# A row roll on one core: the last 256 rows copied in DMAs of half a row per engine

## The chip, the cores and the metric

The kernel runs on one core of a Trainium2 chip. The metric is the device time in microseconds; lower is better. The kernel does almost no computing (in the profile before, VectorE is busy for 1% of the span and GpSimd for 4%): it moves an array within device memory, and 16 DMA engines do the work (each DMA of the copy has 16 landings in the trace). SyncE and ScalarE (SP and ACT in the profile) only issue DMAs; the page lists no busy time for either.

## The reference

```python
x = np.random.randn(8192, 8192).astype(np.float32)
shift = 100
def reference(x, shift):
    return np.roll(x, shift, axis=1)
```

Each row of 32 KiB moves right by 100 elements, and the last 100 elements come round to the front.

## The kernel before

Columns 256 to 8191 of the output (7936 elements, 31744 B per row) are copied straight from input to output. The loop below issues this. The first 256 columns go through on-chip memory on GpSimd's queue.

```python
    engines = [nc.sync, nc.scalar]
    # ... (cut; the comments here and below are the document's)
    # here s = 100, a = 256, g = a - s = 156
    xm = x.rearrange("(c e j) w -> c j e w", e=16, j=4)
    om = out.rearrange("(c e j) w -> c j e w", e=16, j=4)
    if a < n_cols:
        for c in range(n_rows // 64):
            for j in range(4):
                engines[j % 2].dma_start(out=om[c, j, :, a:], in_=xm[c, j, :, g:n_cols - s])
    # ... (the first 256 columns, through GpSimd's queue)
```

Each DMA has an outer dimension of 16. 512 such DMAs are issued, 256 per queue, and the trace has 8192 packets of 31744 B for them and 16 landings for each DMA. This document reads that as one row for each of the 16 DMA engines, though the records do not name the engines. In the trace the 512 DMAs use eight semaphores in turn, 64 DMAs each. All but the first eight wait for their own semaphore, and each of these starts 0.016 to 0.021 us after the last of the 16 landings of the DMA before it on that semaphore. So **eight DMAs are under way** at most. This document calls that the window. Its width in bytes is eight times what one DMA holds.

## Time and profile before

| | kernel before |
|---|---|
| median of the first three runs | 821.17 us (819.21 to 822.31) |
| span of the profiled run | 818.3 us |
| rate in the second half of the span, the last two slices of 40 left out | 326 to 341 GB/s |
| a DMA, issue to landing, median | 12.6 us |
| a row on one engine with its semaphore write, mean; the quickest row alone | 1.477 us; 1.173 us |

The prediction below shows the lines and reads them. The *skew* of a DMA is the time from its first landing to its last: the trace records 16 landings for each DMA, up to 8.1 us apart in the last 16 DMAs of the kernel before. The *end* is the end of the last data packet, 1.3 to 1.9 us before the end of the span in all traces.

### The profile page before, as it was taken

Reading aid. Unit: us, or ns where it says so; the run is one execution under the profiler, and the core shown is the slowest. Engines: PE = TensorE matmul, PEld = TensorE weight load, DVE = VectorE, ACT = ScalarE, POOL = GpSimd, SP = SyncE. Lnnn points to the kernel's source line nnn. Section 1 sums busy time; section 2 is a strip of 40 time slices with the busy share of each in tenths; the row PEclk is TensorE's granted clock in tenths of the full one; section 3 lists DMA queues with packets and bytes.
Section 4 is the critical chain, followed back from the end, with each engine's and each line's share of the span. In section 5 each row is a group of like instructions: output and inputs, shape, how many; then the busy total and the mean of one; then the engine's idle time right before and its main releaser. Section 6 shows DMA issues by size and latency. Waiting matters only on the chain. (4 is left out here: it accounts for less than half of the span.)

```text
span 818.3 us, 617 instructions
## 1 busy us (share of the span) xinstructions
DVE 7.7 (1%) x8; POOL 28.8 (4%) x40
## 2 busy tenths in 40 slices
DVE  0000000000000000000000000000000000000000
POOL 3000000000000000000000000000000000000000
DMA  9999999999999999999999999999999999999997
GB/s 313 343 345 352 338 352 342 363 338 358 349 342 352 354 355 352 348 364 357 337 335 341 327 335 334 326 332 334 338 337 334 330 334 334 332 327 334 334 321 262
DMA packets 21060, 276.89 MB, mean 338 GB/s; under 512 B 8768, under 2 KB 8768, under 8 KB 12864
## 3 DMA queue, kind: packets, MB, share of 16 engines
q10 hardware_dynamic: 8192, 130.04, 46.4%
q1 hardware_dynamic: 8192, 130.04, 46.0%
q0 software_dynamic: 4672, 16.78, 6.8%
q14 instruction: 4, 0.03, 0.0%
HBM read 268.44 MB, written 268.44 MB: 656 GB/s over the span
## 5 line engine op out<-in xcount | busy, mean ns | idle before, releaser
L77 POOL DMA_DIRECT2D out_dram<-h x16 | 13.2, 825 | 197.8 <-DMA out_dram<-h 112.6
L68 POOL DMA_DIRECT2D t<-in_x_dram x12 | 9.5, 793 | 59.7 <-DMA h<-in_x_dram 30.0
L70 DVE COPY h<-t 128x1200 f32<-128x1200 f32 x4 | 3.1, 786 | 232.3 <-DMA t<-in_x_dram 173.4
L73 DVE COPY h<-t 128x1872 f32<-128x1872 f32 x4 | 4.9, 1224 | 0.0
L69 POOL DMA_DIRECT2D h<-in_x_dram x4 | 3.0, 748 | 45.4 <-DMA t<-in_x_dram 45.4
L72 POOL DMA_DIRECT2D h<-in_x_dram x4 | 3.0, 750 | 41.7 <-DMA t<-in_x_dram 41.7
L94 POOL MEMSET const-float32-0.0<- 128x1 f32 x1 | 0.1, 98 | 0.2 <-issue 0.2
L94 POOL MEMSET const-bfloat16-1.0<- 128x1 bf16 x1 | 0.1, 102 | 0.0
L94 POOL MEMSET const-uint8-127<- 128x1 uint8 x1 | 0.1, 99 | 0.0
L94 POOL MEMSET const-float32-1.0<- 128x1 f32 x1 | 0.1, 98 | 0.0
## 6 DMA issues: line engine op xcount, KB each, us to landing
out_dram<-in_x_dram ACTq DMA_DIRECT2D x256, 496.0 KB, 12.6
out_dram<-in_x_dram SPq DMA_DIRECT2D x256, 496.0 KB, 12.6
out_dram<-h POOLq DMA_DIRECT2D x16, 512.0 KB, 113.7
t<-in_x_dram POOLq DMA_DIRECT2D x12, 512.0 KB, 94.9
h<-in_x_dram POOLq DMA_DIRECT2D x4, 312.0 KB, 92.1
h<-in_x_dram POOLq DMA_DIRECT2D x4, 200.0 KB, 97.4
```

Source lines behind the costliest of these rows:

```text
L68: nc.gpsimd.dma_start(out=t[:, q - 1], in_=lead)
L69: nc.gpsimd.dma_start(out=h[:, Q - 1, :, :s], in_=xt[k, Q - 1, :, :, n_cols - s:])
L70: nc.vector.tensor_copy(h[:, :Q - 1, :, :s], t[:, :, :, :s])
L72: nc.gpsimd.dma_start(out=h[:, 0, :, s:], in_=xt[k, 0, :, :, :g])
L73: nc.vector.tensor_copy(h[:, 1:, :, s:], t[:, :, :, s:])
L77: nc.gpsimd.dma_start(out=ot[k, q, :, :, :a], in_=h[:, q])
L94: nc = _bacc.Bacc("TRN2", target_bir_lowering=False, num_devices=1)
```

## The change

It is meant to level the finish. In the profiled run of the kernel before, eight engines end from 811.2 to 812.7 us, and the other eight still have rows to move until 814.7 to 816.8 us. Smaller DMAs at the end are meant to let the quick engines run ahead by less.

The diff is shown without its unchanged lines.

```diff
-        for c in range(n_rows // 64):
+        blocks = n_rows // 64
+        mid = (a + n_cols) // 256 * 128
+        for c in range(blocks):
+            parts = ((a, mid), (mid, n_cols)) if c >= blocks - 4 and a < mid else ((a, n_cols),)
             for j in range(4):
-                engines[j % 2].dma_start(out=om[c, j, :, a:], in_=xm[c, j, :, g:n_cols - s])
+                for lo, hi in parts:
+                    engines[j % 2].dma_start(out=om[c, j, :, lo:hi], in_=xm[c, j, :, lo - s:hi - s])
```

## The prediction

Its sum: -0.9 us for the more level end and +0.3 us for the packets, -0.6 us together. Its 8 ns per packet are the estimate from the quickest packets in the trace (158 ns for 4096 B, 1173 ns for 31744 B); its 2.3 us fixed are one from the 4.7 us to the first landing, less two packets. The 1 us per turn of the window under rival 2, and with it 824.5 us, is the author's guess; no trace gives it.

> **What bounds the kernel now.** I read the page first, then the longest waits of the SyncE queue, then the issues of the copy loop (line 38), and last the stretches of the end.
>
> ```profile
> span 818.3 us, 617 instructions
> ...
> DMA  9999999999999999999999999999999999999997
> GB/s 313 343 345 352 338 352 342 363 338 358 349 342 352 354 355 352 348 364 357 337 335 341 327 335 334 326 332 334 338 337 334 330 334 334 332 327 334 334 321 262
> ...
> q10 hardware_dynamic: 8192, 130.04, 46.4%
> q1 hardware_dynamic: 8192, 130.04, 46.0%
> q0 software_dynamic: 4672, 16.78, 6.8%
> ```
>
> The DMA engines are busy in 39 of 40 slices, and the compute engines do next to nothing, so the transfers are the bound. In the last half, where only the copy loop moves data, the rate is 326 to 341 GB/s. The last slice alone has holes: 7 tenths and 262 GB/s. The change touches only what happens there and shortly before. The two hardware queues hold 8192 packets each; by size these are 4096 rows of 31744 B and 4096 semaphore writes of 4 B, so a whole row is one packet. Its mean time is (46.4% + 46.0%) x 818.3 us x 16 engines / 8192 rows = 1.477 us. The packet records give 1.173 us for the quickest, so a row takes a quarter longer while all 16 engines run than it could.
>
> ```profile
> SPq L38 <- DMA out_dram<-in_x_dram: 670.4, 252, 3.9
> SPq L108 <- DMA out_dram<-in_x_dram: 10.7, 4, 3.1
> ...
> L38 ACTq DMA_DIRECT2D out_dram<-in_x_dram x256: 516/517/828, 0.7 to 806.0; - x128
> L38 SPq DMA_DIRECT2D out_dram<-in_x_dram x256: 509/510/627, 0.7 to 805.8; - x128
> ...
> DMA to landing us min/median/max: 5.6/12.6/14.9
> ```
>
> The queue waited 252 times, which is 256 issues less the first four. The order of instructions says why: each DMA waits for one of eight semaphores, four on SyncE's queue and four on ScalarE's, so exactly eight DMAs are under way. Two of them, one per queue, are finished every 3.1 us or so, hence the 12.6 us from issue to landing. Issue costs 0.51 us of these 3.1, and the sequencer is not the bound.
>
> ```profile
> core 0: us, DVE busy (x) POOL busy (x), PEclk, DMA share, GB/s
> 794.00:800.00 6.00, 0.00 (x0) 0.00 (x0) 1.00 1.04 328
> 800.00:806.00 6.00, 0.00 (x0) 0.00 (x0) 1.00 1.01 339
> 806.00:811.20 5.20, 0.00 (x0) 0.00 (x0) 1.00 0.93 317
> 811.20:812.80 1.60, 0.00 (x0) 0.00 (x0) 1.00 0.65 278
> 812.80:814.70 1.90, 0.00 (x0) 0.00 (x0) 1.00 0.43 184
> 814.70:816.80 2.10, 0.00 (x0) 0.00 (x0) 1.00 0.18 76
> 816.80:818.30 1.50, 0.00 (x0) 0.00 (x0) 1.00 0.00 0
> ```
>
> This is the tail that the change aims at. The landing records show that every DMA has its 16 landings spread out: in the last 50 us the first comes some 5 us after the issue and the last some 12.7 us after it, a skew of 6.2 to 8.2 us. Chaining the packets end to start gives each engine's own end: eight engines end from 811.2 to 812.7 us, the other eight from 814.7 to 816.8 us. Summed over the engines that is 42.6 engine-us of idling, 2.66 us of the whole machine. After 812 us the packets left take 1.175 us each, the quickest time: with half the engines silent, the rest run at full speed. The last four pairs of DMAs land 3.2, 2.4 and 2.3 us apart, where 3.1 was usual before.
>
> [...]16 landings per DMA, up to 8 us apart, and the next issue starts 0.02 us after the last one. So the eight-DMA window moves at the pace of the slowest engine, and limits how far a quick one can run ahead.
> [...]the quickest 4096 B packet took 158 ns, the quickest 31744 B packet 1173 ns, so (1173 - 158) / 27648 B is 0.0367 ns per byte, and 158 - 150 leaves about 8 ns per packet.
> [...]both queues' DMAs of a pair land 0.2 us apart on the slow engines.
> [...]16 engines at 31744 B per 1.173 us would be 433 GB/s, and the steady copy makes 335. Something shared holds the engines back, and that is what decides what a more level finish is worth.
>
> **The change, part by part.** *Removed:* the last 16 DMAs of 496 KB (8 per queue). *Added:* 32 DMAs of 248 KB (16 per queue). The bytes, their order, the queue of each row and the addresses stay. The split falls at 4224, so both halves are 3968 elements, 15872 B. The order of instructions shows the same eight semaphores in the same turn. The part concerned is 256 rows x 31744 B = 8.13 MB, 24.3 us at 335 GB/s, so about from 792 us to the end; nothing before that changes.
>
> *Cost, packets.* Each engine gets 16 more data packets at 8 ns and 16 more semaphore writes, whose median record is 9 ns: 16 x 17 ns = 0.27 us, on the path of the slowest engine.
> *Cost, issues.* 16 x 0.51 us = 8.2 us per queue within 24 us, where a DMA is due every 1.55 us. Hidden.
> *Cost, thinner window.* Eight half DMAs are 8 x 15872 B per engine; on a slow engine that is 8 x 0.78 = 6.2 us of work. When the oldest pair lands there, three pairs, 4.6 us, are still queued. The first packet of the program starts 1.4 us after the first issue, so a new DMA reaches it in time and the slow engine never starves. Cost 0.
> *Gain, tail.* The lead of a quick engine is bounded by the window. Issue to first landing now is 4.7 us or so, of which two packets are 2.4 us and the rest 2.3 us fixed; with halves that is 2.3 + 1.2 = 3.5 us, against 6.2 us for the slowest. So the skew should fall from 6 to 8 us to about 2.7 us, and the 5.6 us from the first engine's end to the last's to about half. What is a fully level end worth? From 811.2 to 816.8 us the engines work (5.6 - 2.66) x 16 = 47 engine-us, which at 1.175 us is 40 rows. All 16 engines at 1.477 us per row do 10.8 rows per us, 3.7 us for the 40: a level end would come 1.9 us sooner. Half the skew: 0.9 us sooner.
> *Sum:* -0.9 + 0.3 = -0.6 us, if the quick engines' new idling costs nothing. Before the end everything stands, and from the last packet to the end of the span is 1.5 us both times. So 821.2 - 0.6 = 820.6; I choose 820.5.
>
> **The rivals.**
> *1. The idling is only moved.* To lose 3 to 5 us of lead, the quick engines must sit idle during those 24 us, waiting for the window, instead of after 811 us. If they all idle at once, the slow ones run at 1.175 us a row then and at 1.477 us at the end, the same sum in another order. For it: the quick engines are a group of eight that ends within 1.5 us, so they would likely stall together. Against: over short stretches the stalls need not coincide, and up to a fifth of the engines could be idle without the shared limit loosening (335/433 is 0.77). It makes the time 821.2 + 0.3 = 821.5.
> *2. The window becomes the bound.* If a new DMA takes much longer than 1.4 us to reach the engines under load (quick engines show 2.3 us fixed in all)[...], halving what is queued starves the slow engines too. Losing 1 us for each of the four turns of the window, the estimate is +3 to +4 us, 824.5. Against: 4.6 us are queued behind each landing.
> *3. Short packets level the sharing.* The two groups may owe their difference to how packets of 31744 B compete; shorter ones could bring all 16 engines to one pace, and the whole 1.9 us would come: 819.5. Nothing speaks for it beyond the level start, where the skew is 0.5 us.
>
> **Range and chances.** The spread of these is 819 to 824.5 us, with most weight at 820 to 821.5. The three times of the kernel before run from 819.21 to 822.31 us, so noise of 1.5 us either way is larger than the effect. I take 817.5 to 823.0. Two per cent are 16.4 us: faster by that is impossible by the sum above, as the whole idle tail is 2.66 us; slower needs the last 24 us to grow by two thirds. Chances: 1% faster, 98% within, 1% slower.
>
> **What would show it.** In the changed kernel: 248 issues per queue of 496 KB and 16 of 248 KB; issue to landing of the halves 6 to 7 us; skew in the halves 2.5 to 4 us; first to last engine's end under 4 us and the rate before the end unchanged at 320 to 340 GB/s. If the DMA share of the 20 us before the tail sinks below 0.95 while the tail gets shorter, rival 1 is right. If the rate of that stretch sinks below 310 GB/s and the span grows, rival 2. If the halves' engines end within 1 us at an unchanged rate, rival 3. The prediction is wrong if the times leave 817.5 to 823.0, or if the skew of the halves stays at 6 us or more, because then the window does not set it.

## More of the kernel before

All runs told here are at a granted clock of 1.0. Chips differ more than kernels do: the kernel before took 820 to 821 us on two chips and 830 to 831 us on two others (medians). So a kernel is compared only with runs of the kernel before on the same chip in the same rounds.

## The result and the profile after

The changed kernel took 819.87 us in the median of six runs (818.34 to 820.66). The kernel before took 820.99 us in six runs (818.13 to 822.31). The ratio is 0.9989 with a 95% interval of 0.9969 to 1.0009. Ratios here are the mean time of one kernel's fast runs over that of the other's in the same rounds, so not quite the ratio of the medians. Within 2%, as predicted, and not clear of zero.

The page of the changed kernel, with the busy tenths of the DMA engines and their rate in 40 slices:

```profile
span 817.9 us, 633 instructions
...
DMA  9999999999999999999999999999999999999998
GB/s 307 333 348 342 347 355 347 355 356 344 350 338 363 359 351 354 361 346 360 334 333 341 326 335 331 331 332 337 328 338 331 330 336 331 335 334 326 331 308 299
```

Look at the last two slices. In the kernel before they read 321 and 262 GB/s; here they read 308 and 299. The last slice gained and the one before it lost.

The issues, with count, size and median time from issue to landing, and the longest waits of SyncE's queue:

```profile
out_dram<-in_x_dram ACTq DMA_DIRECT2D x248, 496.0 KB, 12.7
...
out_dram<-in_x_dram SPq DMA_DIRECT2D x16, 248.0 KB, 5.7
out_dram<-in_x_dram ACTq DMA_DIRECT2D x16, 248.0 KB, 5.9
```

```profile
SPq L43 <- DMA out_dram<-in_x_dram: 671.1, 259, 3.9
SPq L113 <- DMA out_dram<-in_x_dram: 5.3, 4, 2.0
```

The halves land after 5.7 and 5.9 us, less than half of the 12.7 us of the whole rows: the window is half as wide, eight times 248 KB instead of eight times 496 KB. The waits at the very end (line 113 here, 108 before) fell from 10.7 to 5.3 us.

Now the same stretches counted back from the end in both kernels. The columns are the stretch, its length, busy time of the compute engines, clock, share of the DMA engines, and GB/s. A packet counts wholly in the stretch in which it starts, so a share can pass 1. The kernel before:

```profile
core 0: us, DVE busy (x) POOL busy (x), PEclk, DMA share, GB/s
784.80:790.80 6.00, 0.00 (x0) 0.00 (x0) 1.00 1.01 323
790.80:798.80 8.00, 0.00 (x0) 0.00 (x0) 1.00 0.94 294
798.80:808.80 10.00, 0.00 (x0) 0.00 (x0) 1.00 1.00 337
808.80:812.80 4.00, 0.00 (x0) 0.00 (x0) 1.00 0.83 310
812.80:816.80 4.00, 0.00 (x0) 0.00 (x0) 1.00 0.30 127
```

The changed kernel:

```profile
784.60:790.60 6.00, 0.00 (x0) 0.00 (x0) 1.00 0.97 317
790.60:798.60 8.00, 0.00 (x0) 0.00 (x0) 1.00 0.79 278
798.60:808.60 10.00, 0.00 (x0) 0.00 (x0) 1.00 0.94 346
808.60:812.60 4.00, 0.00 (x0) 0.00 (x0) 1.00 0.99 337
812.60:816.60 4.00, 0.00 (x0) 0.00 (x0) 1.00 0.74 242
```

The hole of the last 4 us is largely filled: the share went from 0.30 to 0.74. A new hole opened where the whole rows turn into halves, at 790 to 799 us, with a share of 0.79. The reading is that the quick engines wait there for the slow ones, because the narrower window no longer lets them stay ahead; e3 and e6 below test it.

### The profile page after: what moved, and what is told of

It is laid out like the page before. It is cut to its first block, busy times and chain, and to the rows that moved or that the text cites. A ratio compares the mean times of both kernels' runs of the same rounds, so it can differ in the third digit from the quotient of the medians.

```text
span 817.9 us, 633 instructions
## 1 busy us (share of the span) xinstructions
DVE 7.7 (1%) x8; POOL 28.9 (4%) x40
## 6 DMA issues: line engine op xcount, KB each, us to landing
out_dram<-in_x_dram ACTq DMA_DIRECT2D x248, 496.0 KB, 12.7
out_dram<-in_x_dram SPq DMA_DIRECT2D x248, 496.0 KB, 12.7
```

## The experiments

Twelve runs were made, all with the right result; five of them are one of the two kernels again. In the diffs, `...` marks lines that are cut. Each value in the table below is from one profiled execution. For e6 the skew is that of the row DMAs alone. "Idle" is time in which the 16 engines had no data packet, averaged over the engines, by the packet records (semaphore writes are left out). "Last 12 MB" is how long before the end 12 MB were still to be moved.

| run | skew of the last 8 DMAs (median) | idle, 40 to 8 us before the end | idle, last 8 us | last 12 MB |
|---|---|---|---|---|
| before, three traces | 6.7, 6.4, 6.7 us | 0.4, 0.5, 0.1 us | 2.9, 3.3, 3.8 us | 39.1, 38.6, 39.9 us |
| changed, first three traces | 1.5, 1.7, 1.8 us | 2.2, 1.2, 1.4 us | 0.8, 0.6, 1.0 us | 37.7, 37.3, 37.8 us |
| e3: half packets, wide window | 5.1 us | 0.1 us | 3.0 us | 39.0 us |
| e6: whole packets, narrow window | 2.2 us | 3.1 us | 1.6 us | 39.7 us |
| e5: halves in the last 128 rows | 2.1 us | 1.4 us | 1.3 us | 37.8 us |
| e2: quarters | 1.6 us | 6.4 us | 2.0 us | 45.1 us |

### e0: the changed kernel again

No edit.

> The changed kernel once more, for a closer interval. My theory after the first look: the eight-DMA window sets the skew between engines; halving it makes the quick engines idle between about 790 and 800 us instead of after 811 us, and only a part of the tail's 2.7 us of idling is won. Ratio to before 0.9985 to 0.9995 (819.8 to 820.6 where before is 821), last engines ending within 1 to 2 us of each other. Rival, all of the gain is noise: 1.000 with the interval on both sides of it.

Measured: 831.31 us against 830.36, ratio 1.0014 (0.9995 to 1.0033). The trace has the expected shape, with a small skew and a hole before the end, but the total time shows no gain on this chip.

### e3: half-size packets, window as wide as before

The change does two things at once: it halves the packet, and it halves the bytes under way. This run does only the first. Each DMA holds two half rows per engine, from two neighbouring rows.

```diff
...
+                if c < blocks - 4:
+                    engines[j % 2].dma_start(out=om[c, j, :, a:], in_=xm[c, j, :, g:n_cols - s])
+                    continue
+                at = (c * 64 + j // 2 * 2) * n_cols + j % 2 * w    # w = 3968
+                engines[j % 2].dma_start(
+                    out=bass.AP(tensor=out.tensor, offset=at + a, ap=[[4 * n_cols, 16], [n_cols, 2], [1, w]]),
+                    in_=bass.AP(tensor=x.tensor, offset=at + g, ap=[[4 * n_cols, 16], [n_cols, 2], [1, w]]))
```

> The last 256 rows in packets of half a row, but two packets per engine and DMA, so that a DMA stays 496 KB and the window stays as wide as in the kernel before. Theory (the window sets the skew, not the packet): skew of the landings stays 5.5 to 8 us, the engines end some 5 us apart, time as before (+0.1 to +0.3 us for 16 more packets). Rival (short packets level the sharing among the engines): skew of 1 to 2.5 us and a level end, as the changed kernel shows.

The stretches of 18 to 8, 8 to 4 and 4 to 0 us before its end:

```profile
811.10:821.10 10.00, 0.00 (x0) 0.00 (x0) 1.00 0.99 333
821.10:825.10 4.00, 0.00 (x0) 0.00 (x0) 1.00 0.96 329
825.10:829.10 4.00, 0.00 (x0) 0.00 (x0) 1.00 0.20 83
```

The tail is that of the kernel before: a share of 0.20 in the last 4 us, 3.0 us of idling in the last 8 us, and a skew of 4.6 to 6.5 us in the last eight DMAs, a little under the 5.5 to 8 us expected. Half-size packets alone do not level the end. The time was 831.93 us, ratio 1.0021 (1.0005 to 1.0038). That is 0.4 to 3.1 us more (0.0005 and 0.0038 times 830.4), where 0.1 to 0.3 us was expected. Why it should be more I did not find out.

### e6: whole packets, narrow window

The opposite. Between two row DMAs a DMA of 512 B per engine takes up a semaphore, so four row DMAs are under way, as many bytes as eight halves. In its trace these row DMAs landed 7.5 us after the issue in the median, where the last whole rows of the kernel before took 12.7 us.

```diff
...
+        sp = spare.tile([16, 16 * 128], x.dtype)
...
                 engines[j % 2].dma_start(out=om[c, j, :, a:], in_=xm[c, j, :, g:n_cols - s])
+                if c >= blocks - 4:
+                    engines[j % 2].dma_start(out=sp[:, n * 128:n * 128 + 128], in_=xm[c, j, :, 0:128])
+                    n += 1
```

> The last 256 rows in whole-row packets, but between two of them a DMA of 512 B per engine that nobody reads, which takes up one of the eight semaphores: four row DMAs under way instead of eight, as many bytes as eight halves. Theory (window): skew of the last row DMAs 2 to 3.5 us, engines end within 2.5 us, holes in the DMA share before the tail; time between 819.5 and 821.5. Rival (packet size): skew stays 5.5 us or more, time as before or a little over.

The stretches of 26 to 18, 18 to 8, 8 to 4 and 4 to 0 us before its end:

```profile
802.20:810.20 8.00, 0.00 (x0) 0.00 (x0) 1.00 0.72 265
810.20:820.20 10.00, 0.00 (x0) 0.00 (x0) 1.00 0.93 310
820.20:824.20 4.00, 0.00 (x0) 0.00 (x0) 1.00 1.04 365
824.20:828.20 4.00, 0.00 (x0) 0.00 (x0) 1.00 0.45 155
```

The hole before the end and a more level end are there with whole packets: 1.6 us of idling in the last 8 us, against 2.9 to 3.8 us in the kernel before. The last eight row DMAs have a skew of 0.9 to 3.6 us. With e3 this settles which of the two counts here: **the bytes in the window set the skew, not the packet.** The skew does not simply follow the bytes, though: halves brought it from 6.4 to 6.7 us down to 1.5 to 2.1 us, and quarters (e2) left it at 1.6 us. The time was 831.68 us, ratio 1.0016 (1.0002 to 1.0030), somewhat worse than expected. The engines were idle for 3.1 us before the tail, against 1.1 to 2.2 us with halves; that this ate up what the tail gave fits the numbers, but was not tested apart.

### e2: quarters of a row

```diff
-            parts = ((a, mid), (mid, n_cols)) if c >= blocks - 4 and a < mid else ((a, n_cols),)
+            parts = [(a + i * w, a + i * w + w) for i in range(4)] if c >= blocks - 4 else [(a, n_cols)]  # w = 1984
```

> The last 256 rows in quarters of a row: 64 DMAs of 124 KB. Theory: eight of them are 8 x 7936 B per engine, some 3.1 us of work at the shared pace, while a DMA needs at least about 2.9 us from issue to its first landing on an idle engine; a turn of the window takes some 3.8 us, 267 GB/s instead of 335, so 30 us for the 8.13 MB instead of 24 us, less 1 to 2 us for a level end: 824 to 827 us, share of the DMA engines 0.6 to 0.8 over the last 30 us. If the window is still wide enough, the time is 820 to 821 and the engines end within 1 us.

Its quarters in the view of the issues, and the stretch of 18 to 8 us before its end:

```profile
out_dram<-in_x_dram SPq DMA_DIRECT2D x32, 124.0 KB, 4.0
```

```profile
817.00:827.00 10.00, 0.00 (x0) 0.00 (x0) 1.00 0.83 260
```

Measured: 836.99 us against 830.36, ratio 1.0079 (1.0060 to 1.0098). A turn of the window took 4.0 us, where 3.8 was expected, and the rate fell to 260 GB/s. Here the window is the bound: at the 333 GB/s of the copy, eight DMAs of 124 KB would turn in 3.1 us, and they took 4.0. The expectation's 2.9 us to the first landing is the prediction's 2.3 us plus two quarters of a row; the last eight quarters had theirs after 2.6 us in the median. The cost, 6.5 us by the ratio, is a little over the 3 to 6 us expected. This is rival 2 of the prediction, one halving further on. That halves are still wide enough is shown by e1 below, where the rate holds; a window's bytes over its landing time can't show it, because that quotient gives about the rate itself whether or not the window is the bound.

### e1: all rows in halves

```diff
-            parts = ((a, mid), (mid, n_cols)) if c >= blocks - 4 and a < mid else ((a, n_cols),)
+            parts = ((a, mid), (mid, n_cols)) if a < mid else ((a, n_cols),)
```

> All 8192 rows in halves, so the thin window holds all the way: no lead is built up and there is no change from one window to the other. Theory (something that the engines share is the bound, and idle engines cost nothing while a few at a time are idle): share of the DMA engines 0.94 to 0.97 throughout, rate as before, engines end within 2 us; the 512 more packets and semaphore writes per engine, 512 x 17 ns = 8.7 us, are hidden in that slack: ratio 0.998 to 1.004. Rival (the slowest engines are the bound, each packet's cost is on the path): 8.7 us more and some 1 us won at the end, ratio 1.008 to 1.012.

The stretches 400 to 600 and 600 to 780 us, in e1:

```profile
400.00:600.00 200.00, 0.00 (x0) 0.00 (x0) 1.00 0.99 333
600.00:780.00 180.00, 0.00 (x0) 0.00 (x0) 1.00 1.00 332
```

In the kernel before:

```profile
400.00:600.00 200.00, 0.00 (x0) 0.00 (x0) 1.00 1.00 334
600.00:780.00 180.00, 0.00 (x0) 0.00 (x0) 1.00 1.00 333
```

The rate is the same within 1 GB/s. The ratio was 1.0020 (0.9994 to 1.0045), 822.85 us against 820.27. The 8.7 us of added packets and semaphore writes, an estimate from the trace before (512 times 17 ns: 8 ns per packet and 9 ns per semaphore write, its median), would be 1.0106. The upper end of the interval is 3.7 us, or 5.3 us if the 1.6 us that a level end is worth in the last 12 MB (below) are added back, so a good part of them is hidden. The share was expected to fall to 0.94 to 0.97; it stayed at 0.98 to 0.99 over most of the run by the packet records.

Two more things are in e1's trace. Between 400 and 780 us the median skew of its DMAs is 1.9 us, where the kernel before has 5.9 us: the window holds the engines together all the way, not only at the end. And one thing changed that was not meant to. GpSimd's part was through by 181 us instead of 485, and its stores landed after 32.5 us in the median instead of 113.7. So e1's total mixes two effects, and the rate from 400 us on is the cleaner evidence.

### e4: eight changes of window instead of one

```diff
-            parts = ((a, mid), (mid, n_cols)) if c >= blocks - 4 and a < mid else ((a, n_cols),)
+            parts = ((a, mid), (mid, n_cols)) if c % 16 >= 12 and a < mid else ((a, n_cols),)
```

> Whole rows for 768 rows, halves for 256, eight times over: the change of window that the changed kernel makes once is made eight times, and the lead of the quick engines, which took some 50 us to build up at the start, has 73 us to come back. If a change of window costs nothing net (idle engines leave their share to the others): ratio 0.999 to 1.003. If each gives up what the idling of the quick engines is worth (rates of 256 and 295 instead of 335 GB/s for 6 us, some 1.1 us, in part regained): 8 x 0.7 to 1.1 us = 6 to 9 us more, less the level end: ratio 1.006 to 1.010.

Measured: 822.93 us against 820.27, ratio 1.0024 (1.0007 to 1.0041), the lower of the two bands. By this ratio eight changes cost 0.6 to 3.4 us together (0.0007 and 0.0041 times 820), so at most some 0.6 us each, even if the 1.6 us that a level end is worth in the last 12 MB (below) are added back: (3.4 + 1.6) / 8. The idling at a change of window seems mostly paid for by the engines that go on. The lead had come back only in part, though: before the eight changes the median skew of the last eight whole-row DMAs was 3.8 to 8.3 us, under 5 us in four of them, so a change from the full lead may cost somewhat more.

### e7: the last 32 rows on eight engines

This tries to level the end without idling before it, by giving more to some engines.

```diff
...
+                if c < blocks - 1 or j < 2:
+                    engines[j % 2].dma_start(out=om[c, j, :, a:], in_=xm[c, j, :, g:n_cols - s])
+                    continue
+                for e in (0, 8):
+                    engines[j % 2].dma_start(out=om[c, j, e:e + 8, a:], in_=xm[c, j, e:e + 8, g:n_cols - s])
```

> Whole rows, wide window as before, but the last 32 rows in four DMAs of 8 rows, which run on eight of the engines alone (four rows each there, none on the others, where before each of the 16 had two). If those eight are the quick ones, which end some 4 us early, the end comes out level without idling before: 1 to 1.9 us sooner, ratio 0.998 to 0.999. If they are the slow ones: their two more rows cost 2 x 1.175 us, ratio 1.003 and a longer tail of half the engines, 6 to 8 us. If quick and slow are mixed among them, in between, near 1.001.

Measured: 822.25 us against 820.27, ratio 1.0021 (1.0004 to 1.0038). By the packet records eight engines were busy until 3.9 us before the end, and four of them until 0.6 us. So the eight are neither all quick nor all slow. The trace of b_before, on the same chip, adds that the split into eight quick and eight slow engines does not hold there: in its last DMA on SyncE's queue 12 engines landed within 2.5 us of the first and four 5.5 to 5.8 us after it. Without records that name the engine, this way was left.

### e5: halves in the last 128 rows only

`c >= blocks - 4` becomes `c >= blocks - 2`.

> Only the last 128 rows in halves. In the changed kernel the skew was down to some 2 us after four to five pairs of halves, so 128 rows (eight pairs) should be enough: engines end within 2.5 us of each other, the holes of the change of window now lie 18 to 6 us before the end, the last 12 MB take 37 to 38.5 us, ratio 0.998 to 1.002. If the thin window has to hold longer than that, the engines still end 4 to 5 us apart and the last 12 MB take 38.5 to 39.5 us.

Measured: 829.79 us against 830.91, ratio 0.9991 (0.9976 to 1.0006). The last 12 MB took 37.8 us, as in the changed kernel. 128 rows are enough to use up the lead.

### b, b2, a2, a3: both kernels again

These give more traces and a narrower ratio.

> The kernel before as a run of its own, for a second trace of it on the chip of these runs: ratio 1.000, and the last 12 MB take 38 to 40 us, engines end some 5 us apart.

> The kernel before a third time, for its trace on the chip of the run of the changed kernel: ratio 1.000, last 12 MB in 38.5 to 39.2 us, engines end 4 to 5.5 us apart.

> The changed kernel a third time, next to a third trace of the kernel before on the same chip. If the level end is worth something: the last 12 MB take 37 to 38 us here and 38.5 to 39.2 us in the kernel before, as in the traces so far (37.7 and 37.3 against 39.1 and 38.6). In the total time this is 0.15% and may stay hidden: ratio 0.997 to 1.002.

> The changed kernel a fourth time, to narrow the ratio. In the traces so far the last 12 MB take 37.3 to 37.8 us in the changed kernel and 38.6 to 39.9 us in the kernel before, 1.6 us less, while the three ratios (0.9989, 1.0014, 0.9993) together say 0.9999 +- 0.0011. If the 1.6 us reach the end: ratio 0.998. If they are made up for elsewhere or are chance: 1.000. The last 12 MB should again take 37 to 38 us.

The kernel before against itself: 1.0000 (0.9979 to 1.0022) and 1.0001 (0.9987 to 1.0015). The engines began to run out some 5 us before its end each time. The changed kernel: 829.89 us, ratio 0.9993 (0.9976 to 1.0011), and 829.13 us, ratio 0.9982 (0.9968 to 0.9996). In the fourth trace of the changed kernel (a3) the last 12 MB took 37.5 us, with 1.1 us idle before and 0.7 us in the tail, and the median skew was 2.1 us.

**All four ratios of the changed kernel together** (0.9989, 1.0014, 0.9993, 0.9982, each weighted by the inverse square of its interval) give 0.9992 with about 0.0009 either way: 0.6 us less, between 1.4 us less and 0.1 us more. This treats the four as independent, though the last two share most runs of the kernel before. They also lie wider apart than chance alone makes likely: 1.0014 and 0.9982 have intervals that hardly touch. Whether the chip matters here stays open.

The ratios of single experiments need the same care. On one chip e0, e3 and e6 came out at 1.0014, 1.0021 and 1.0016, on another e1, e4 and e7 at 1.0020, 1.0024 and 1.0021, though these kernels do quite different things. All ratios of one chip share the same runs of the kernel before, so a chance shift of those would move them together. A difference of 0.2% in one ratio is therefore not put down to an edit here.

**In the last 12 MB the gain is plainer.** Three traces of the kernel before give 39.2 us in the mean, four of the changed kernel 37.6 us, 1.6 us less, and the two groups do not overlap. With three and four traces, a difference of 0.9 us is not excluded. Whether all of it reaches the end stays open, because the rest of the run varies by more than that between executions.

No version that clearly beats both kernels came out: e5 is as good as the change and no better.

## Why the prediction was right

**The time.** 820.5 was forecast, with 98% on "within 2%"; 819.87 was measured. The sum of -0.6 us agrees with the pooled -0.6 us, which is luck in part, as the interval, some 0.7 us either way, is larger than the effect.

**The bound.** That something shared limits the engines, not each engine its own work, is supported by e1, where 8.7 us of added engine work did not move the rate, and by the tail before, where rows took 1.175 us once half the engines were silent. What it is that they share was not tested; the page of the kernel before has 656 GB/s read and written together in device memory over the span. Three readings of the prediction were a little off: early in the last half it is not only the copy loop that moves data (GpSimd's last packet ends at 485 us), the slice before the last, at 321 GB/s, lies outside the 326 to 341 given, and the skew in the last 50 us goes down to 5.6 us, not 6.2, with the last pair.

**The window sets the skew.** Right, and shown by the pair e3 and e6, with e1 for the middle of a run. The size was off: 2.7 us was forecast, with a mark of 2.5 to 4 us, and medians of 1.5 to 2.1 us were measured in four traces. The term that was mis-sized is the first landing: 3.5 us after the issue was forecast, and the last four halves on SyncE's queue, from which the forecast's figure came, had it after 3.9 to 4.5 us in the median of each of the four traces. Their last landing came after 5.6 to 6.2 us, where 6.2 was forecast. The forecast's two even groups of eight engines were also those of one trace: b_before had four late engines, not eight. The finish became more level than forecast: of 16 engines, 15 were busy until 1.0 us before the end in the first trace, where I expected up to 4 us between first and last.

**The thinner window costs nothing.** Right for halves. The change of window was felt for some 8 us, and after it the rate was 346 GB/s over 10 us. e2 shows how near the limit is: one more halving of the same 256 rows makes the whole run 0.8% longer.

**The tail's gain of 0.9 us and rival 1.** The truth lies between them. The mark that I set for rival 1 was met: from 790.6 to 812.6 us, before the tail, the share was 0.90 (the three stretches shown, weighted by length), below 0.95, with 0.79 in the first 8 us. Averaged over the traces (three before, four changed), idling in the last 8 us fell from 3.3 to 0.8 us, and idling 40 to 8 us before the end rose from 0.4 to 1.5 us. So 2.5 us were taken away and 1.1 us came back earlier; not quite half was only moved. What remains, 1.4 us of idling, lies nearer to the 1.6 us won in the last 12 MB than the forecast's 0.9 us does, though 0.9 us is not excluded either. Rival 1 as stated, with no gain at all, fails in the last 12 MB; in the total time it is not excluded, as the pooled interval reaches 0.1 us more. e4 points the same way: eight changes of window cost less than the 6 to 9 us that full payment would have been.

**The packets' cost of 0.27 us on the path.** This term has no support. The cost on an engine is real: the quickest half row took 589 ns, and twice that is 5 ns more than the quickest whole row's 1173 ns, where the forecast had 8 ns. (The forecast took its figure from GpSimd's 4096 B packets, which go to or from on-chip memory.) But e1 shows that much of such a cost stays off the path: at most 5.3 of the 8.7 us showed there. e3, on the other hand, was 0.4 to 3.1 us slower with only 16 more per engine, which is more than that cost could be, 0.27 us.

**Rival 3** falls with e3: short packets in a wide window leave the skew at 5.1 us.

## What to carry to other kernels

In these runs eight DMAs were under way and each waited for the complete landing of an earlier one. The bytes in that window set how far the quick engines ran ahead of the slow ones: 6.4 to 6.7 us of skew with whole rows, 1.5 to 2.1 us with halves. Cutting the last DMAs shorter levelled the finish, but part of the idling returned where the window narrowed (1.1 of 2.5 us), and with quarters the rate fell to 260 instead of 333 GB/s. Size and bytes under way changed together in e2, so whether more DMAs of 124 KB under way would hold the rate was not tested. What holds for another kernel has to be read from its own trace: the time from issue to landing, the skew and the DMA share. Before levelling a tail, work out its whole worth: here it was 2.7 us of idling in 820 us, so even a perfect finish was below half a per cent.
